# Columns of a folded layer norm inside the main matmuls, and the index scores of three row tiles in one go

## The chip, the cores and the metric

The kernel runs on one core of one Trainium2 chip. Six engines matter here: PE (TensorE) multiplies matrices, DVE (VectorE), ACT (ScalarE) and POOL (GpSimd) work on tiles, SP (SyncE) issues most transfers, and the DMA engines move data between HBM and the on-chip memory SBUF. PE writes into PSUM, which has eight banks of 512 float32 columns on 128 partitions. The metric is the device time of one execution in microseconds (us); 2847.55 us is the median of three runs of the kernel before.

## The reference, cut

Two transformer blocks run one after the other over 512 rows of 1024 columns. In the first one every normalized result goes at once into a product:

```python
def layer_norm(x, g, b):
    mu = mean(x); var = mean((x - mu) ** 2)
    return (x - mu) * rsqrt(var + LN_EPS) * g + b

for i in range(2):
    h = layer_norm(ALPHA * h + 0.5 * swiglu(h, w1, w3, w2), ...)
    mix = ab_mixer(h @ ab_w_in) if i == 0 else dsa_mixer(h @ c_w_in)
    h = layer_norm(ALPHA * h + mix @ w_out, ...)
    h = layer_norm(ALPHA * h + 0.5 * swiglu(h, w1, w3, w2), ...)
    h = h + (p[i] @ ple_w_proj[i]) * sigmoid(h @ ple_w_gate[i])
```

The second mixer picks, for each row, the keys that it attends to by an index of eight small heads (`q` and `k` pass through a rotation, "rope", first):

```python
logits = relu(einsum('bthd,bsd->bths', qi, ki))     # 8 heads of 64
score = einsum('bths,bth->bts', logits, wi)         # weighted sum over heads
score = where(causal, score, -inf)
idx = top_k(score, 128)                             # per row
```

The second block (three attentions and 32 experts, of which each row uses two) is not touched.

## The kernel before, in words

Activations lie transposed: eight tiles of 128 channels by 512 rows (`DT` is 8, `P` 128, `S` 512). Every float32 product is made of three matmuls: each operand is split into a high part and the rest (`hi`, `lo`), and `mm3` (L261 to L263) adds high x high, high x low and low x high in a PSUM bank. `w` loads a weight of 128 x 1024, ScalarE casts the high part (L238), DVE, or POOL where `low` says so, subtracts it (L239); both go into rings of six.

`first_products` is called six times: at the start of the two mixers, in the two second feed-forwards (`ffn`) and in the two gates (`ple`). It starts four products before the layer norm of their input is known. `gained` has prepared `G`, the input times the gain as a pair of tiles, one pair for each of the eight channel tiles. A `part(i, k)` is the product of output i with channel tile k: three matmuls of 512 columns into `out[i]` and two small ones (L412, L413), with the gain and bias vectors themselves as moving columns (four and two), into a shared bank `cs`. `pair(0)` runs outputs 0 and 1 over k, with the sums of the norm (L312, L313: 16 matmuls of one column) after k = 3. DVE turns the sums into the factors of the norm (`rstd`, `rsqrt`: L324 to L356, L338), builds two diagonal tiles from them (L372), and `spread` multiplies these by ones (L374), so that the factors stand in a row for all partitions; ScalarE copies that out (L375). `pair(2)` runs outputs 2 and 3. `corrected` puts the norm in after the fact: out times the first row (L433), and the column sums from `cs` (L436 on ScalarE, L437 on DVE) times the second row added (L439). `normed` makes the normalized input itself, `H`, as pairs (L391, L392, L393, L394), for the products that follow.

In `c_mixer` the generator `index` makes the scores of row tiles 3, 2 and 1 (512, 384 and 256 keys): for each of eight heads a matmul (L1041), a rectifying ScalarE operation into an SBUF tile (L1043) and a multiply-add on DVE (L1045, L1047), then sixteen rounds of top-k on DVE (L1054, L1055). It is interleaved with ten projections and their rope: per projection a ScalarE copy (L970), a shuffle on DVE (L971) and three products on POOL (L973 to L975). From the third projection on, two steps of `index` follow each. The heads (L1084, L1127, L1144) need the result.

The instructions of each engine run in the order in which a scheduler has put the program's; engines meet by semaphores. Buffers come from pools: `self.t()` is one of `SLOTS` (53) tiles of 256 KB, `self.bank()` one of eight PSUM banks. At the end of the program the experts' weights are loaded into the same slots, by SP, in order (L1622, L1625 are its waits there).

Of the kernel before, what the change touches and what calls it, by code (L numbers as in the profile page):

```python
# [9 lines left out]
F32 = mybir.dt.float32  # L10
F32R = mybir.dt.float32r
I32 = mybir.dt.int32
BF16 = mybir.dt.bfloat16
AF = mybir.ActivationFunctionType
ALU = mybir.AluOpType
# [4 lines left out]
S = 512  # L20
D = 1024
DT = D // P
# [27 lines left out]
C_I32, C_BASE, C_TOK, C_I128 = 640, 672, 736, 768  # L50
SLOTS, RING, S5_STEP = 53, 6, 2
CAP, NCOL, NPAIR, NEXT = 64, 32, 16, 16
# [87 lines left out]
class K:  # L140
# [236 lines left out]

    def gained(self, y, g):

        nc, (hi, lo) = self.nc, (self.t(F32R), self.t(F32R))  # L380
        gain = self.vec[:, g:g + 1]
        nc.scalar.activation(hi, y, AF.Copy, scale=gain)  # L382
        nc.vector.scalar_tensor_tensor(lo, y, gain, hi.bitcast(F32), op0=ALU.mult, op1=ALU.subtract)
        return hi, lo
# [12 lines left out]
    def first_products(self, ws, norm, late=False, use=None):  # L397
# [6 lines left out]
        ws, n = list(ws), 4  # L404
        cs, out = self.bank(), [self.bank() for _ in range(n)]

        def part(i, k):
            s = slice(k * P, (k + 1) * P)
            hi, lo = (w[:, s] for w in ws[i])
            v, at = self.gains[:, 4 * (g - V_LNG + k):], 8 * i  # L410
            self.mm3(out[i], (hi, lo), G[k], k == 0, k == DT - 1)
            mm(cs[:, at:at + 4], hi, v[:, :4], start=i == 0 and k == 0, stop=False)  # L412
            mm(cs[:, at:at + 2], lo, v[:, :2], start=False, stop=i == n - 1 and k == DT - 1)  # L413
            self.last_mm = self.mark()
# [14 lines left out]
        def corrected():  # L429
            res, c, ts = [], self.sm(8 * n), []  # L430
            for o in out:
                t = self.t()
                nc.vector.tensor_tensor(t, o, rows[0], ALU.mult)  # L433
                ts.append(t)
            v = lambda t: t[:, :8 * n].rearrange("p (i c) -> p i c", c=8)
            nc.scalar.copy(v(c)[:, :, 2:4], v(cs)[:, :, 2:4])  # L436
            nc.vector.tensor_tensor(v(c)[:, :, 0:2], v(cs)[:, :, 0:2], v(c)[:, :, 2:4], ALU.add)  # L437
            for i, t in enumerate(ts):
                nc.vector.scalar_tensor_tensor(t, rows[1], c[:, 8 * i:8 * i + 1], t, op0=ALU.mult, op1=ALU.add)  # L439
                res.append((t, c[:, 8 * i + 1:8 * i + 2]))  # L440
                if use:
                    use(i, *res[-1])
            return res
# [21 lines left out]
    def ffn(self, X, H, i, ln, then=None, ws=None):  # L465
# [4 lines left out]
        for pi, (a, b) in enumerate(FF_PARTS):  # L470
# [31 lines left out]
            for d in range(DT):  # L502
# [5 lines left out]
                if last:  # L508
                    G.append(self.gained(Y[d], V_LNG + ln * 8 + d))
                    self.stat_add(st, Y[d])  # L510
                    if d == 1 and then:
                        then()
# [16 lines left out]
    def mix_out(self, X, wname, xs, ln, low=None):  # L529
        nc, st, Y, G = self.nc, {}, [], []  # L530
        for d in range(DT):
# [3 lines left out]
            Y.append(y)  # L535
            G.append(self.gained(y, V_LNG + ln * 8 + d))
            self.stat_add(st, y)
        return Y, (Y, G, st, V_LNG + ln * 8, V_LNB + ln * 8)

    def ple(self, X, norm, i, g=None):  # L540
# [13 lines left out]
        for d in range(DT):  # L554
# [10 lines left out]
            if g is not None:  # L565
                HY.append(self.gained(y, g + d))
                self.stat_add(st, y, mean=False)
            else:
                HY.append(self.split(y))
# [418 lines left out]
    def c_mixer(self, X, H):  # L988
# [44 lines left out]
        def index():  # L1033
            for j in (3, 2, 1):
                n = (j + 1) * P
                acc = self.t()[:, :n]
                for h in range(8):
# [3 lines left out]
                    nc.tensor.matmul(o[:, :n], q[rs, j * P:(j + 1) * P], ki[rs, :n], start=True, stop=True)  # L1041
                    r = self.t()
                    nc.scalar.activation(r[:, :n], o[:, :n], AF.Relu)  # L1043
# [25 lines left out]
        for n, _ in enumerate(self.rounds([self.rope(product, ra, sh_a, 32, (nc.gpsimd, nc.gpsimd), qk, n) for n in range(10)], 1)):  # L1069
            for _ in range(2 if n > 1 else 0):  # L1070
                next(idx, None)
# [945 lines left out]
```

## Time and profile before

| what | value |
|---|---|
| median of three runs | 2847.55 us (2846.9 to 2848.05) |
| the profiled execution | 2847.58 us |
| its span, first to last instruction | 2845.8 us |
| PE busy | 2721.4 us, 96% |
| DVE busy | 1545.7 us, 54% |
| ACT busy | 998.7 us, 35% |
| POOL busy | 238.5 us, 8% |
| mean granted clock of PE | 0.968 |

Busy time is the time in which at least one instruction of the engine runs. Matmuls are pipelined, so the records of two that follow one another overlap: their pace is read from the distance of their starts, not from the length of one. The granted clock is 1 at 2.4 GHz and 0.5 at 1.2 GHz. In a row of the timeline the bracket at the end is the idle time of the engine ahead of it and the instruction that ended it.

### The profile page before, as it was taken

Reading aid. Unit: us, or ns where it says so; the run is one execution under the profiler, and the core shown is the slowest. Engines: PE = TensorE matmul, PEld = TensorE weight load, DVE = VectorE, ACT = ScalarE, POOL = GpSimd, SP = SyncE. Lnnn points to the kernel's source line nnn. Section 1 sums busy time; section 2 is a strip of 40 time slices with the busy share of each in tenths; the row PEclk is TensorE's granted clock in tenths of the full one; section 3 lists DMA queues with packets and bytes.
Section 4 is the critical chain, followed back from the end, with each engine's and each line's share of the span. In section 5 each row is a group of like instructions: output and inputs, shape, how many; then the busy total and the mean of one; then the engine's idle time right before and its main releaser. Section 6 shows DMA issues by size and latency. Waiting matters only on the chain. (4 is left out here: it accounts for less than half of the span.)

```text
span 2845.8 us, 34267 instructions
## 1 busy us (share of the span) xinstructions
PE 2721.4 (96%) x13091; PEld 2130.7 (75%) x13091; DVE 1545.7 (54%) x2873; ACT 998.7 (35%) x1634; POOL 238.5 (8%) x250
## 2 busy tenths in 40 slices
PE   9999999999999999999996799999999999969996
PEld 7888878888888878888875588888887777754443
DVE  6856364565333564333579765333578766553435
ACT  5332243334222363222342434222356544322111
POOL 2101001000000000000025000000014222010000
PEclk9999998999999999999998899999999999989998
DMA  6434215423233323223220223232223222669993
GB/s 216 160 109 143 91 58 165 157 93 104 95 98 92 100 78 104 95 91 97 88 104 23 74 67 111 94 99 89 94 100 106 95 74 83 220 208 369 405 410 138
DMA packets 123814, 369.97 MB, mean 130 GB/s; under 512 B 14592, under 2 KB 14656, under 8 KB 123648
## 3 DMA queue, kind: packets, MB, share of 16 engines
q1 hardware_dynamic: 112688, 333.10, 35.1%
q0 software_dynamic: 10384, 33.61, 3.0%
q8 instruction: 103, 1.69, 0.2%
q10 hardware_dynamic: 576, 1.05, 0.1%
q14 instruction: 63, 0.52, 0.1%
HBM read 343.32 MB, written 24.39 MB: 129 GB/s over the span
## 5 line engine op out<-in xcount | busy, mean ns | idle before, releaser
L261 PE MATMUL p<-a,wh 128*128 128x512 f32 x3008 | 1197.4, 399 | 9.4 <-ACT a L551 5.7
L262 PE MATMUL p<-a,wh 128*128 128x512 f32 x3008 | 1178.1, 392 | 1.2 <-DVE a L394 1.2
L263 PE MATMUL p<-a,wl 128*128 128x512 f32 x3008 | 1176.4, 391 | 0.0
L238 ACT CAST wh<-wr 128x1024 fp32r<-128x1024 f32 (+2 forms) x399 | 409.5, 1033 | 1114.4 <-PE p L262 736.5
L261 PEld LDWEIGHTS p<-a,wh 128*128 128x128 f32 x3008 | 569.6, 189 | 135.2 <-issue 7.1
L263 PEld LDWEIGHTS p<-a,wl 128*128 128x128 f32 x3008 | 568.5, 189 | 120.4 <-issue 0.2
L262 PEld LDWEIGHTS p<-a,wh 128*128 128x128 f32 x3008 | 569.5, 189 | 117.7 <-issue 2.6
L239 DVE TENSOR_TENSOR wl<-wr,wh 128x1024 fp32r<-128x1024 f32 (+2 forms) x394 | 471.8, 1201 | 330.2 <-ACT wh L238 319.6
L497 DVE TENSOR_TENSOR a<-a,p 128x512 f32<-128x512 f32 x84 | 57.8, 688 | 262.1 <-PE p L263 244.5
L507 DVE SCALAR_TENSOR_TENSOR a<-p,a 128x512 f32<-128x512 f32 x96 | 66.3, 691 | 192.7 <-PE p L263 192.7
L787 POOL DMA_DIRECT2D spill<-a x76 | 42.6, 562 | 1410.0 <-DVE a L563 556.8
L1134 ACT ACTIVATE a<-a,s 128x256 f32<-128x256 f32 (+3 forms) x128 | 67.4, 528 | 95.3 <-DVE s L1132 95.1
L256 DVE TENSOR_TENSOR a<-a,a 128x512 fp32r<-128x512 f32 x128 | 88.6, 698 | 16.4 <-ACT a L255 16.0
L255 ACT CAST a<-a 128x512 fp32r<-128x512 f32 x128 | 78.5, 622 | 28.8 <-DVE a L563 10.5
L391 DVE TENSOR_TENSOR a<-a,a 128x512 f32<-128x512 f32 x96 | 60.0, 685 | 13.6 <-ACT a L375 13.6
L1846 PE MATMUL p<-we,a 128*64 128x512 f32 x288 | 63.7, 592 | 0.0
L1885 PE MATMUL p<-a,sel 128*128 128x512 f32 x256 | 61.0, 394 | 0.1
L382 ACT ACTIVATE a<-a,vec 128x512 fp32r<-128x512 f32 x56 | 40.5, 723 | 54.0 <-DVE a L507 27.9
L1869 ACT ACTIVATE a<-p,wgt 128x512 fp32r<-128x512 f32 x32 | 22.0, 689 | 103.6 <-PE p L1867 100.0
L1127 DVE CUSTOM_DVE_ANT_0 a<-p,a 128x256 f32<-128x256 f32 (+3 forms) x120 | 50.4, 462 | 11.3 <-PE p L1283 11.0
L1885 PEld LDWEIGHTS p<-a,sel 128*128 128x128 f32 x256 | 47.3, 188 | 11.0 <-issue 0.8
L1886 DVE TENSOR_TENSOR a<-a,p 128x512 f32<-128x512 f32 x72 | 48.4, 686 | 12.6 <-PE p L1885 12.2
(442 smaller groups left out, 2561.3 us busy)
## 6 DMA issues: line engine op xcount, KB each, us to landing
wr<-in_w_dram SPq DMA_DIRECT2D x204, 512.0 KB, 3.4
we<-in_wgu_dram SPq DMA_DIRECT2D x72, 512.0 KB, 9.4
wr<-in_w_dram SPq DMA_DIRECT2D x64, 448.0 KB, 3.3
a<-in_wgu_dram SPq DMA_DIRECT2D x112, 256.0 KB, 5.6
spill<-a POOLq DMA_DIRECT2D x76, 256.0 KB, 2.5
a<-spill SPq DMA_DIRECT2D x76, 256.0 KB, 6.0
we<-in_wd_dram SPq DMA_DIRECT2D x36, 512.0 KB, 11.2
wr<-in_win_dram SPq DMA_DIRECT2D x31, 512.0 KB, 3.8
```

What stands on the lines that cost most here:

```text
L238: nc.scalar.copy(hi[:, :n], raw[:, :n])
L239: (low or nc.vector).tensor_tensor(lo[:, :n], raw[:, :n], hi[:, :n].bitcast(F32), ALU.subtract)
L255: self.nc.scalar.copy(hi[:, :n], x)
L256: (low or self.nc.vector).tensor_tensor(lo[:, :n], x, hi[:, :n].bitcast(F32), ALU.subtract)
L261: mm(o, l[0], r[0], start=start, stop=False)
L262: mm(o, l[0], r[1], start=False, stop=False)
L263: mm(o, l[1], r[0], start=False, stop=stop)
L391: nc.vector.tensor_tensor(y, y, row, op)
L507: nc.vector.scalar_tensor_tensor(Y[d], o, 0.5, Y[d], op0=ALU.mult, op1=ALU.add)
L1134: nc.scalar.activation(s[x], s[x], AF.Exp, bias=nm[:, x:x + 1], accum_out=z[:, x:x + 1])
L1846: nc.tensor.matmul(o[CAP * i:CAP * i + CAP], xT[k // 4][:, a:a + CAP], wg[k], start=k == 0, stop=k == DT - 1)
L1885: nc.tensor.matmul(o, sels[b][:n, j * P:(j + 1) * P], y[h][i][:n], start=b + i == 0, stop=i == 1 and b == len(blocks) - 1)
```

## The change

Norm columns. `gained` now makes its high part as two tiles of 512 columns: `first` holds columns 0 to 255 of the product and, at 256 to 259, the four gain and bias columns, which POOL copies there; the other half goes into a tile that two consecutive channel tiles share. The low part stays one tile. A `part` is six matmuls: three into `out[i]` (260, 256 and 258 columns, so that the four sums come out behind the first 256 columns) and three of 256 columns into a half of a second bank, shared by two outputs. The small matmuls and the bank `cs` are gone; six banks instead of five are held. `corrected` works output by output: two multiplications of 256 columns, a copy of two columns (L454), an addition, the multiply-add. The gate that feeds the second block keeps the old `gained` under the name `gained_rms`. `SLOTS` goes from 53 to 58, for which the room of the descriptors of software DMA is halved.

Index. The rectified scores stay in PSUM (`r = o`), where DVE reads them; and all three row tiles' scores are made behind the second projection, before the third, instead of two tiles behind the third and one behind the fourth.

```diff
-SLOTS, RING, S5_STEP = 53, 6, 2
+SLOTS, RING, S5_STEP = 58, 6, 2
...
-    def gained(self, y, g):
+    def gained(self, y, g, G):
+        nc = self.nc
+        first, lo = self.t(F32R), self.t(F32R)
+        second = G[-1][3] if len(G) % 2 else self.t(F32R)
+        room = second[:, len(G) % 2 * 256:len(G) % 2 * 256 + 256]
+        gain = self.vec[:, g:g + 1]
+        nc.gpsimd.tensor_copy(first[:, 256:260], self.gains[:, 4 * (g - V_LNG):4 * (g - V_LNG) + 4])
+        for hi, s in ((first[:, :256], slice(0, 256)), (room, slice(256, S))):
+            nc.scalar.activation(hi, y[:, s], AF.Copy, scale=gain)
+            nc.vector.scalar_tensor_tensor(lo[:, s], y[:, s], gain, hi.bitcast(F32), op0=ALU.mult, op1=ALU.subtract)
+        G.append((first, room, lo, second))
+
+    def gained_rms(self, y, g):
         nc, (hi, lo) = self.nc, (self.t(F32R), self.t(F32R))
...
-        cs, out = self.bank(), [self.bank() for _ in range(n)]
+        out, second = [self.bank() for _ in range(n)], [self.bank() for _ in range(n // 2)]
+        place = lambda i: second[i // 2][:, i % 2 * 256:i % 2 * 256 + 256]
...
-            self.mm3(out[i], (hi, lo), G[k], k == 0, k == DT - 1)
-            mm(cs[:, at:at + 4], hi, v[:, :4], start=i == 0 and k == 0, stop=False)
-            mm(cs[:, at:at + 2], lo, v[:, :2], start=False, stop=i == n - 1 and k == DT - 1)
+            wh, wl = (w[:, s] for w in ws[i])
+            a, b, lo, _ = G[k]
+            o, begin, end = out[i], k == 0, k == DT - 1
+            mm(o[:, :260], wh, a[:, :260], start=begin, stop=False)
+            mm(o[:, :256], wh, lo[:, :256], start=False, stop=False)
+            mm(o[:, :258], wl, a[:, :258], start=False, stop=end)
+            o, begin, end = place(i), begin and i % 2 == 0, end and i % 2 == 1
+            mm(o, wh, b, start=begin, stop=False)
+            mm(o, wh, lo[:, 256:], start=False, stop=False)
+            mm(o, wl, b, start=False, stop=end)
             self.last_mm = self.mark()
...
-            res, c, ts = [], self.sm(8 * n), []
-            for o in out:
-                t = self.t()
-                nc.vector.tensor_tensor(t, o, rows[0], ALU.mult)
-                ts.append(t)
...
-            nc.scalar.copy(v(c)[:, :, 2:4], v(cs)[:, :, 2:4])
-            nc.vector.tensor_tensor(v(c)[:, :, 0:2], v(cs)[:, :, 0:2], v(c)[:, :, 2:4], ALU.add)
...
+            for i in range(n):
+                t, c = self.t(), self.sm(4)
+                nc.vector.tensor_tensor(t[:, :256], out[i][:, :256], rows[0][:, :256], ALU.mult)
+                nc.vector.tensor_tensor(t[:, 256:], place(i), rows[0][:, 256:], ALU.mult)
+                nc.scalar.copy(c[:, 2:4], out[i][:, 258:260])
+                nc.vector.tensor_tensor(c[:, 0:2], out[i][:, 256:258], c[:, 2:4], ALU.add)
+                nc.vector.scalar_tensor_tensor(t, rows[1], c[:, 0:1], t, op0=ALU.mult, op1=ALU.add)
+                res.append((t, c[:, 1:2]))
...
-                    r = self.t()
+                    r = o
                     nc.scalar.activation(r[:, :n], o[:, :n], AF.Relu)
...
-            for _ in range(2 if n > 1 else 0):
+            for _ in range((0, 3)[n] if n < 2 else 2):
                 next(idx, None)
...
-    nc = bacc.Bacc("TRN2", target_bir_lowering=False, num_devices=1)
+    nc = bacc.Bacc("TRN2", target_bir_lowering=False, num_devices=1, dynamic_dma_scratch_size=8192)
```

Three places show what the change does to the order in which instructions stand on an engine. The first is PE at the start of `pair(0)` in the `ab_mixer` stage. In the kernel before, with `a_2828` and `a_2829` the pair of channel tile 0, `wh_3095` and `wl_3096` the weight of output 0, `p_3118` the bank `cs`:

```order
L261 MATMUL p_3119<-a_2828,wh_3095 128x512
L262 MATMUL p_3119<-a_2829,wh_3095 128x512
L263 MATMUL p_3119<-a_2828,wl_3096 128x512
L412 MATMUL p_3118<-gains,wh_3095 128x4
L413 MATMUL p_3118<-gains,wl_3096 128x2
L261 MATMUL p_3120<-a_2828,wh_3101 128x512
```

And now, with `a_2828` the first half and the four columns, `a_2830` the second half, `a_2829` the low part, `p_3150` the second bank:

```order
L426 MATMUL p_3146<-a_2828,wh_3123 128x260
L427 MATMUL p_3146<-a_2829,wh_3123 128x256
L428 MATMUL p_3146<-a_2828,wl_3124 128x258
L430 MATMUL p_3150<-a_2830,wh_3123 128x256
L431 MATMUL p_3150<-a_2829,wh_3123 128x256
L432 MATMUL p_3150<-a_2830,wl_3124 128x256
L426 MATMUL p_3147<-a_2828,wh_3129 128x260
```

Five matmuls have become six, none of them small. In the kernel before, the 32 small ones of `pair(2)` all stood between the end of `pair(0)` and the spread (L374); now nothing does.

The second place is ScalarE in the same stage, behind the copies of the spread rows. In the kernel before (L392 makes the normalized tiles, L878 and L806 belong to the mixer and use the outputs, L393 casts the first `H`):

```order
L375 COPY a_3244<-p_3243 128x512
L392 ACTIVATE a_258<-a_258,vec 128x512
L392 ACTIVATE a_260<-a_260,vec 128x512
L392 ACTIVATE a_262<-a_262,vec 128x512
L392 ACTIVATE a_264<-a_264,vec 128x512
L392 ACTIVATE a_266<-a_266,vec 128x512
L392 ACTIVATE a_268<-a_268,vec 128x512
L392 ACTIVATE a_270<-a_270,vec 128x512
L878 ACTIVATE a_3343<-a_3332,s_3331 128x512
L878 ACTIVATE a_3346<-a_3334,s_3331 128x512
L878 ACTIVATE a_3349<-a_3336,s_3331 128x512
L806 COPY wr_3422<-p_3423 64x512
```

L878 for the fourth output and then L393 follow. Now, from the last L405 (the former L392) on, where `p_3148` and `p_3149` are the banks of outputs 2 and 3 and L895, L823, L406 are the former L878, L806, L393:

```order
L405 ACTIVATE a_270<-a_270,vec 128x512
L454 COPY s_3411<-p_3148 128x2
L823 COPY wr_3496<-p_3497 64x512
L405 ACTIVATE a_272<-a_272,vec 128x512
L823 COPY wr_3496<-p_3503 64x512
L895 ACTIVATE a_3417<-a_3410,s_3411 128x512
L454 COPY s_3420<-p_3149 128x2
L831 COPY wr_3553<-wr_3496 64x1024
L238 CAST wh_3591<-wr_3590 128x1024
L895 ACTIVATE a_3426<-a_3419,s_3420 128x512
L406 CAST a_3428<-a_258 128x512
```

The first cast of `H` stands, before and now, behind work on the outputs of `pair(2)`; the small copies of each output (L454) have come into this row.

The third place is DVE where the index begins. In the kernel before three shuffles of the rope stand ahead of the scores, which read SBUF tiles (`a_10977` and so on, which ScalarE has written):

```order
L971 STREAM_SHUFFLE a_10895<-a_10894 32x512
L971 STREAM_SHUFFLE a_10933<-a_10932 32x512
L971 STREAM_SHUFFLE a_10971<-a_10970 32x512
L1045 TENSOR_SCALAR a_10974<-a_10977,s_10845 128x512
L1047 SCALAR_TENSOR_TENSOR a_10974<-a_10982,s_10845,a_10974 128x512
```

Now two stand there, and the scores read PSUM banks (`p_`):

```order
L988 STREAM_SHUFFLE a_11191<-a_11190 32x512
L239 TENSOR_TENSOR wl_11199<-wr_11197,wh_11198 128x1024
L988 STREAM_SHUFFLE a_11229<-a_11228 32x512
L1062 TENSOR_SCALAR a_11232<-p_11233,s_11141 128x512
L1064 SCALAR_TENSOR_TENSOR a_11232<-p_11237,s_11141,a_11232 128x512
```

The third shuffle now stands behind the scores of all three row tiles and the first two rounds of top-k.

## Rows read from the trace of the kernel before

**Rows 1.** The page, part 1: busy time, share and instructions of each engine.

```profile
PE 2721.4 (96%) x13091; PEld 2130.7 (75%) x13091; DVE 1545.7 (54%) x2873; ACT 998.7 (35%) x1634; POOL 238.5 (8%) x250
```

**Rows 2.** Windows of the six stages: us; busy of PE, PEld, DVE, ACT, POOL; PEclk, DMA.

```profile
380.54:418.48 37.94, 37.48 (x181) 30.59 (x179) 22.84 (x53) 10.85 (x16) 1.63 (x3) 0.87 0.20 70
...
sum 219.33, PE 218.87 PEld 180.85 DVE 136.00 ACT 73.08 POOL 4.88; mean PE 36.48 PEld 30.14 DVE 22.67 ACT 12.18 POOL 0.81
```

**Rows 3.** Timeline of PE, `pair(0)` of the first stage: start, length, instruction.

```profile
381.36 0.48 PE L261 MATMUL p<-a,wh 128*128 128x512 f32 x1
381.68 0.40 PE L262 MATMUL p<-a,wh 128*128 128x512 f32 x1
381.91 0.39 PE L263 MATMUL p<-a,wl 128*128 128x512 f32 x1
...
382.28 0.48 PE L261 MATMUL p<-a,wh 128*128 128x512 f32 x1
...
387.76 0.36 PE L312 MATMUL p<-ones,a 128*128 128x1 f32 x2
```

**Rows 4.** Timeline of PE, first stage: burst of small matmuls and the spreads.

```profile
398.45 0.25 PE L412 MATMUL p<-gains,wh 128*128 128x4 f32 x1
...
403.35 2.06 PE L374 MATMUL p<-a,ones 128*128 128x512 f32 x2
405.86 1.87 PE L374 MATMUL p<-a,ones 128*128 128x512 f32 x2 [0.46 <-DVE a L372]
```

**Rows 5.** Timeline of PE, matmuls of 264 columns in `c_mixer`.

```profile
1454.81 0.28 PE L261 MATMUL p<-wh,a 128*128 128x264 f32 x1
...
1455.30 0.28 PE L261 MATMUL p<-wh,a 128*128 128x264 f32 x1
```

**Rows 6.** The page, part 5: busy and mean ns of a group, then idle time before.

```profile
L238 ACT CAST wh<-wr 128x1024 fp32r<-128x1024 f32 (+2 forms) x399 | 409.5, 1033 | 1114.4 <-PE p L262 736.5
L261 PEld LDWEIGHTS p<-a,wh 128*128 128x128 f32 x3008 | 569.6, 189 | 135.2 <-issue 7.1
```

**Rows 7.** Timeline of DVE, first stage: factors of the norm, and the two diagonals.

```profile
389.72 0.16 DVE L324 TENSOR_SCALAR s<-p 128x4 f32<-128x4 f32 x1 [4.81 <-PE p L313]
...
394.04 0.87 DVE L372 TENSOR_SCALAR a<-const,s 128x128 f32<-128x128 f32 x4
403.72 0.17 DVE L437 TENSOR_TENSOR s<-p,s 128x8 f32<-128x8 f32 x1 [8.81 <-ACT s L436]
...
404.94 0.87 DVE L372 TENSOR_SCALAR a<-const,s 128x128 f32<-128x128 f32 x4
```

**Rows 8.** Timeline of PE, first stage: the first product with `H`.

```profile
422.50 0.49 PE L261 MATMUL p<-a,wh 128*128 128x512 f32 x1 [2.19 <-ACT a L393]
```

**Rows 9.** Timeline of DVE, `c_mixer`: shuffles of the rope and the scores.

```profile
1483.88 0.72 DVE L971 STREAM_SHUFFLE a<-a 32x512 f32<-32x512 f32 x1
...
1490.00 4.33 DVE L1045 TENSOR_SCALAR a<-a,s 128x512 f32<-128x512 f32 x1
1494.44 12.68 DVE L1047 SCALAR_TENSOR_TENSOR a<-a,s,a 128x512 f32<-128x512 f32 x7
...
1509.88 3.50 DVE L1047 SCALAR_TENSOR_TENSOR a<-a,s,a 128x384 f32<-128x384 f32 x5
...
1515.93 6.53 DVE L1047 SCALAR_TENSOR_TENSOR a<-a,s,a 128x256 f32<-128x256 f32 x7
```

**Rows 10.** Timeline of PE, `c_mixer`: the wait ahead of the heads.

```profile
1580.59 2.47 PE L1567 MATMUL p<-const,a 128*128 128x128 f32 x10 [41.45 <-DVE a L1144]
```

**Rows 11.** Timeline of DVE and POOL in the second block, working at one time.

```profile
2151.83 3.54 POOL L1254 TENSOR_TENSOR a<-a,old 128x512 f32<-128x512 f32 x2 [23.28 <-DVE old L1243]
...
2154.81 0.69 DVE L256 TENSOR_TENSOR a<-p,a 128x512 fp32r<-128x512 f32 x1 [0.59 <-ACT a L255]
```

**Rows 12.** Waits of SP's queue ahead of the experts: what for, total, times, longest.

```profile
SPq L1622 <- DMA hfd<-a: 13.4, 1, 13.4
```

**Rows 13.** The page, part 2: GB/s that DMA moved, in 40 slices.

```profile
GB/s 216 160 109 143 91 58 165 157 93 104 95 98 92 100 78 104 95 91 97 88 104 23 74 67 111 94 99 89 94 100 106 95 74 83 220 208 369 405 410 138
```

More of the change, by code (lines that the diff above doesn't have):

```diff
@@ L404, in first_products @@
         ws, n = list(ws), 4
-        cs, out = self.bank(), [self.bank() for _ in range(n)]
+        out, second = [self.bank() for _ in range(n)], [self.bank() for _ in range(n // 2)]
+        place = lambda i: second[i // 2][:, i % 2 * 256:i % 2 * 256 + 256]
         def part(i, k):
             s = slice(k * P, (k + 1) * P)
-            hi, lo = (w[:, s] for w in ws[i])
-            v, at = self.gains[:, 4 * (g - V_LNG + k):], 8 * i
-            self.mm3(out[i], (hi, lo), G[k], k == 0, k == DT - 1)
-            mm(cs[:, at:at + 4], hi, v[:, :4], start=i == 0 and k == 0, stop=False)
-            mm(cs[:, at:at + 2], lo, v[:, :2], start=False, stop=i == n - 1 and k == DT - 1)
+            wh, wl = (w[:, s] for w in ws[i])
[8 more added lines that the diff above has]
+            mm(o, wl, b, start=False, stop=end)
             self.last_mm = self.mark()
@@ L429, in corrected @@
         def corrected():
-            res, c, ts = [], self.sm(8 * n), []
-            for o in out:
-                t = self.t()
-                nc.vector.tensor_tensor(t, o, rows[0], ALU.mult)
-                ts.append(t)
-            v = lambda t: t[:, :8 * n].rearrange("p (i c) -> p i c", c=8)
-            nc.scalar.copy(v(c)[:, :, 2:4], v(cs)[:, :, 2:4])
-            nc.vector.tensor_tensor(v(c)[:, :, 0:2], v(cs)[:, :, 0:2], v(c)[:, :, 2:4], ALU.add)
-            for i, t in enumerate(ts):
-                nc.vector.scalar_tensor_tensor(t, rows[1], c[:, 8 * i:8 * i + 1], t, op0=ALU.mult, op1=ALU.add)
-                res.append((t, c[:, 8 * i + 1:8 * i + 2]))
+            res = []
+            for i in range(n):
[6 more added lines that the diff above has]
+                res.append((t, c[:, 1:2]))
                 if use:
@@ L508, in ffn @@
                 if last:
-                    G.append(self.gained(Y[d], V_LNG + ln * 8 + d))
+                    self.gained(Y[d], V_LNG + ln * 8 + d, G)
                     self.stat_add(st, Y[d])
@@ L535, in mix_out @@
             Y.append(y)
-            G.append(self.gained(y, V_LNG + ln * 8 + d))
+            self.gained(y, V_LNG + ln * 8 + d, G)
             self.stat_add(st, y)
@@ L565, in ple @@
             if g is not None:
-                HY.append(self.gained(y, g + d))
+                HY.append(self.gained_rms(y, g + d))
                 self.stat_add(st, y, mean=False)
```

## The prediction

> **What bounds the kernel now.** I read the busy times first: PE, the matrix engine, is busy for 96% of the span [rows 1], so in most of the program what PE issues is the time. That share is a mean, and the change touches two kinds of place, so I then read those two. In the six runs of `first_products` the windows from the first matmul on `G` to the last matmul of `pair(2)` add to 219.33 us, with PE busy for 218.87 of it, and the granted clock of the first of them is 0.87 [rows 2]: PE is the limit there, and runs part of the time at 1.2 instead of 2.4 GHz. The timeline of PE in the first window shows what the time is made of. Matmuls of 512 columns start 227 ns apart (381.68, 381.91); one `part`, three of these and two small ones, repeats every 0.92 us (381.36, 382.28) [rows 3]. Three times 0.227 is 0.68, so the two small matmuls, six columns together, take 0.24 us of each part. For `pair(2)` the small matmuls stand in a burst of their own, since they need no `G`: 32 of them from 398.45 to 403.35, 4.9 us, and only then the first spread [rows 4]. The last things to read in this stage are the waits around it: DVE waits 8.81 us for the ScalarE copy of `cs` and with it the second diagonal (404.94) [rows 7], and behind `pair(2)` PE waits 2.19 us for the first normed `H` [rows 8].
>
> The other place is the index of `c_mixer`. There PE is not the limit: it waits 41.45 us for DVE before the heads [rows 10], so the time is what DVE does from the third shuffle on: scores, then sixteen rounds of top-k. The scores of the first row tile are the odd rows: 4.33 us for one multiplication of 512 columns, 12.68 for the seven behind it, while five of 384 columns take 3.50 a little later [rows 9]. POOL runs rope and weight splits at that time.
>
> **The change part by part.** *The parts of the six stages.* Removed: two small matmuls in each of 32 parts of a stage. Three matmuls become six of 256 to 260 columns. The nearest row is the one of 264 columns with the same 128x128 weights: five starts within 1454.81 to 1455.30, 0.122 us apart [rows 5]. Six of these are 0.73 us; by columns (258 of 264) 0.71. I take 0.71; the bounds are 0.68, three of 512 columns, and 0.73. `pair(0)`, 16 parts, goes from 16 x 0.92 = 14.7 to 11.4 us. `pair(2)` goes from 16 x 0.68 = 10.9 to 11.4, which is a loss of 0.5. The burst, 4.9 us in the first stage, is gone. The low clock in the windows is another part: 14.7 + 1.8 for the sums (387.76 to the DVE row at 389.72) + 4.9 + about 3.6 for spreads and the wait between them + 10.9 = 35.9, of 37.94 [rows 2, 3, 4, 7]; the 2 us left over is matmuls of `pair(0)` at 1.2 GHz. The granted clock falls there behind the one-column sums and inside the burst. I take it that without the small ones it stays up.
>
> *What is late next in a stage.* With T0 the first matmul: the sums stand after eight parts, at T0 + 5.7 to 7.5. DVE's chain from the first `rstd` step to the end of the first diagonal takes 389.72 to 394.91 [rows 7], 5.2 us, so the first spread may start at T0 + 12.9, while PE gets to it at 11.4 + 1.8 = 13.2: hidden, with 0.3 to spare. The second diagonal stands in DVE's row behind one split of a new weight (L239), which needs the cast of that weight (L238, 1.03 us [rows 6]) into a ring slot that only the end of `pair(0)` frees. So: 13.2 + 1.03 + 1.22 for the split (403.72 to 404.94) + 0.87 for the diagonal [rows 7] = 16.3. The small copies that stood in this row too (L436 and L437) are gone. The second spread ends 0.9 later (half of the 1.87 that two took at the low clock [rows 4]), at 17.2, and `pair(2)` at T0 + 28.6. Six stages: 219.33 - 6 x 28.6 = 47.7 us.
>
> *What of it is given back.* PE then needs `H`, and ScalarE casts the first `H` behind work on the outputs of `pair(2)` (the order above shows it): this wait moves with the end of `pair(2)` and does not grow by the whole gain. But `corrected` is now longer: per output two multiplications instead of one, a copy on ScalarE and an addition on DVE, for the last two outputs some 4 x 0.2 us and two handovers. I take 1.0 us in each stage, 6 in all; the bounds of one stage are 0 and 4 (the whole chain of spread, product, cast late by half of what PE gained). So the stages give 41.7.
>
> *`gained`.* Two halves on ScalarE and DVE for one each and a POOL copy of four columns, 48 times. They stand behind the last product of the stage before, where DVE and ScalarE wait for PE; POOL has 8% busy time [rows 1] and no queue at these places. PE takes tile k of `G` at T0 + 1.4k, and the last one has 10 us. Nothing, and 0.3 us each stage if this cover were gone.
>
> *Index.* Three things. The scores start behind the second shuffle (ends at 1484.6), not the third (which ends where the first score starts, 1490.0): 5.4 us, less one more shuffle of 0.7 that now comes behind them [rows 9]. Second, the rows themselves: those of 512 columns take 4.33 + 12.68 = 17.0 us, seven of 256 columns 6.53, more than the five of 384 suggest [rows 9]. What ails the long ones is seen where POOL and DVE run together elsewhere: with POOL busy from 2151.83 to 2155.37, a DVE operation of 512 columns with one operand in PSUM takes 0.69 us [rows 11]: it is not stretched. The new score operations read PSUM and one SBUF tile, as that one does. For 512 columns I take 0.80 (between this 0.69 and 3.50 / 5 x 512 / 384 = 0.93, which holds the waits of a chain), 0.50 for 256; 384 stay at 0.70. That is 17.0 - 8 x 0.80 = 10.6 less and 6.53 - 7 x 0.50 = 3.0 less, together 13.6 (12 to 15). Third, PE: its eight remaining projections, 24 matmuls of 0.227 us each, 5.45 us, now start some 12 us later (8 x 2.0 = 16 us of scores, less the eight banks that PE may be ahead, 8 x 0.5), near 1497, and end near 1541; the heads now start at 1580.59, and by this at 1562. PE's wait shrinks to some 21 us and still covers them. Sum: 5.4 - 0.7 + 13.6 = 18.3.
>
> *Slots.* Weights of the experts are loaded into the same slots, and SP waits there, once 13.4 us, for a slot [rows 12] before a stretch in which DMA is the limit at about 410 GB/s [rows 13]. Five more slots of 256 KB are 1.3 MB, 3.2 us at that rate, if all of them are filled earlier. 0 to 3.2; I take 2. The smaller ring for software DMA descriptors I cost at nothing; such transfers are few and far apart here.
>
> *Sum.* The profiled execution took 2847.58 us with a span of 2845.8, the median of the runs is 2847.55: the same. 2847.6 - 41.7 - 18.3 - 2 = 2785.6; I say **2786**.
>
> **The rivals.** *Given back behind `pair(2)`.* The DVE and ScalarE rows of `corrected` and `normed`, not PE, set when the next products can start. For it: PE waits for `H` already now [rows 8], and this row is not shorter than before. Against it: the first spread comes at T0 + 13.2 instead of 22.8 (403.35 less 380.54 [rows 2, 4]), and those rows can begin with it. If half is lost, 3.5 us more in each stage: 2786 + 21 = **2807**.
>
> *The scores are still slow.* They go on PE's, ScalarE's or POOL's pace, and the 13.6 us are not had, only the earlier start: **2800**. For it: in no row of before does a chained multiply-add with a PSUM operand run beside POOL's shuffled rope; against it: [rows 11].
>
> *Weight loads set the pace, and the kernel becomes slower.* Six loads instead of five, and half as many columns behind each to hide one. A load's record is 189 ns long [rows 6]. Should each matmul wait for its own, a part is 6 x 0.189 = 1.13 us: `pair(0)` is then 3.4 us longer, `pair(2)` 7.2, the burst saves 4.9, so +5.7 a stage and +34 in all, against 20.3 from index and slots: **2861**. It decides the sign from about 0.176 us a matmul on, where 32 parts of 1.06 us less the 30.5 that parts and burst take now are 3.4 us a stage, 20.3 in all. Against it stands 0.122 at 264 columns [rows 5], with loads as large as these. The Trainium skill has a rule that speaks for this rival (TensorE: Matmul & The Clock Gate, section The mechanism): a weight load overlaps with matmuls in flight only where it goes to another group of rows, and these loads take all rows. By its prices (sections LDWEIGHTS and Back-to-back issue gap) a load of 128 is 107 ns and a matmul of 256 columns 109, so by estimate 216 ns each and 1.30 us a part, and the sum near 2895. This case's trace does not agree: at 0.122 the load is hidden.
>
> *Better than forecast.* The low clock behind PE's waits for `H` goes too, nothing is given back, and all slots count: 47.7 + 20 + 3.2 and some 3 for the clock, **2774**.
>
> *The change does nothing*, if the small matmuls had only filled time in which PE would have waited for the first spread: 2845. Against it: [rows 3], where the 0.24 us lie between full matmuls.
>
> **How the numbers follow.** Forecast 2786: 0.60. Given back, 2807: 0.18. Scores slow, 2800: 0.12. Better, 2774: 0.05. Weight loads, 2861: 0.03. Nothing: 0.02. The range from 2771 to 2810 takes in the first four with the bounds of their terms, and leaves out the other two and the case in which two losses add (about 2820). A difference under 0.2%, 5.7 us, is about what a measurement of this kernel can't tell from none. Faster 0.95, same 0.02, slower 0.03.
>
> **What would show it.** Right: in the new PE timeline parts of 0.71 us with starts 0.118 apart, no burst, windows of 28 to 29.5 us each, clock near 1 in them; the first score at the second shuffle, scores of 512 columns under 1 us with POOL busy, and PE's wait before the heads at 20 to 25 us. Wrong: starts 0.16 or more apart; a wait for `H` of more than 5 us behind `pair(2)`; DVE waiting in the score chain for ScalarE or PE; low clock in the windows all the same.

## The result, and the profile after

The changed kernel took 2785.35 us (median of four runs, 2784.17 to 2786.86) against 2847.63 us: a ratio of 0.9782, with a 95% interval from 0.9765 to 0.9799. Its profiled run took 2784.83 us, with a span of 2782.9.

The same windows as in [rows 2], from the first matmul on `G` to the last of `pair(2)`, in the changed kernel (length in us; busy time of PE, PEld, DVE, ACT, POOL with the number of instructions; granted clock, DMA share, GB/s):

```profile
379.92:408.05 28.13, 26.60 (x213) 25.29 (x212) 23.17 (x58) 12.28 (x20) 1.62 (x3) 1.00 0.29 95
...
sum 168.97, PE 159.59 PEld 151.68 DVE 138.99 ACT 81.56 POOL 4.86; mean PE 26.60 PEld 25.28 DVE 23.16 ACT 13.59 POOL 0.81
```

Together 168.97 us for 219.33. The clock is 1.00 in all six. What stands in a window is seen in the timeline of PE in the first of them, which answers to [rows 3] and [rows 4]:

```profile
390.98 0.28 PE L426 MATMUL p<-a,wh 128*128 128x260 f32 x1
391.10 0.28 PE L427 MATMUL p<-a,wh 128*128 128x256 f32 x1
...
391.69 0.28 PE L426 MATMUL p<-a,wh 128*128 128x260 f32 x1
...
393.12 1.02 PE L374 MATMUL p<-a,ones 128*128 128x512 f32 x2
395.67 1.13 PE L374 MATMUL p<-a,ones 128*128 128x512 f32 x2 [1.53 <-DVE a L372]
396.24 0.68 PE L426 MATMUL p<-a,wh 128*128 128x260 f32 x1
...
414.20 0.80 PE L261 MATMUL p<-a,wh 128*128 128x512 f32 x1 [5.11 <-ACT a L406]
```

A part is 0.71 us (390.98 to 391.69), the first spread starts 13.20 us after the window does, the second waits 1.53 us for DVE, and `pair(2)` begins at T0 + 16.3. The last row answers to [rows 8]: behind `pair(2)` PE now waits 5.11 us for `H`, where it waited 2.19 (and 1.0 more in three short waits beside that row).

The index, as DVE ran it (answers to [rows 9]):

```profile
1448.49 0.71 DVE L988 STREAM_SHUFFLE a<-a 32x512 f32<-32x512 f32 x1
1449.11 0.72 DVE L1062 TENSOR_SCALAR a<-p,s 128x512 f32<-128x512 f32 x1
1449.93 4.17 DVE L1064 SCALAR_TENSOR_TENSOR a<-p,s,a 128x512 f32<-128x512 f32 x5
...
1456.61 2.42 DVE L1065 TENSOR_TENSOR a<-a,const 128x128 f32<-128x128 f32 x1
...
1473.53 0.01 DVE L988 LOAD_MASK_SELECT a<-a  x1 [1.23 <-ACT a L987]
```

And PE ahead of the heads (answers to [rows 10]):

```profile
1529.79 2.47 PE L1584 MATMUL p<-const,a 128*128 128x128 f32 x10 [15.25 <-DVE a L1161]
```

The multiply-adds of 512 columns, 1.8 us each in the kernel before, are 0.83 us apart. From the end of the window in `c_mixer` to the heads it is 112.35 us (1417.44 to 1529.79) instead of 128.02 (1452.57 to 1580.59).

Where the 62.9 us of the span went can be read by laying the matmuls of the two traces side by side. The start of the first window is 0.6 us earlier. The six windows give 9.8, 7.9, 9.4, 9.4, 6.1 and 7.8 us, in sum 50.4. Between the first and the second window 2.1 us are lost again (1.2 in the trace of the repeated run of this kernel below), and between the others that don't hold the index 0.9 more are gained in sum. The stretch with the index, up to the fifth window, gives 15.1. Behind the sixth window 2.0 are lost: 2.1 more are gained right behind it, 2.4 are lost in the attentions of the second block, and 1.6 before the experts, where PE waits for the first gather of rows. That wait was 7.47 us before; in the trace of the changed kernel it is this row:

```profile
2492.82 1.97 PE L1849 MATMUL p<-const,wr 128*128 128x128 f32 x8 [9.10 <-DMA wr<-hfd,toki]
```

Through the whole stretch of the experts the two traces then run at one distance, 62.8 to 63.0 us.

### The profile page after: what moved, and what is told of

Same layout as the page of the kernel before. It is cut to its first block, busy times and chain, and to the rows that moved or that the text cites. A ratio compares the mean times of both kernels' runs of the same rounds, so it can differ in the third digit from the quotient of the medians.

```text
span 2782.9 us, 34941 instructions
## 1 busy us (share of the span) xinstructions
PE 2670.1 (96%) x13283; PEld 2104.5 (76%) x13283; DVE 1543.1 (55%) x2963; ACT 1007.5 (36%) x1700; POOL 251.2 (9%) x298
## 5 line engine op out<-in xcount | busy, mean ns | idle before, releaser
L261 PE MATMUL p<-a,wh 128*128 128x512 f32 x2816 | 1107.4, 394 | 10.7 <-ACT a L406 5.1
L262 PE MATMUL p<-a,wh 128*128 128x512 f32 x2816 | 1101.0, 391 | 0.1
L263 PE MATMUL p<-a,wl 128*128 128x512 f32 x2816 | 1099.3, 391 | 0.0
L239 DVE TENSOR_TENSOR wl<-wr,wh 128x1024 fp32r<-128x1024 f32 (+2 forms) x394 | 472.8, 1203 | 322.0 <-ACT wh L238 312.4
L261 PEld LDWEIGHTS p<-a,wh 128*128 128x128 f32 x2816 | 531.6, 189 | 129.3 <-ACT a L568 5.5
L263 PEld LDWEIGHTS p<-a,wl 128*128 128x128 f32 x2816 | 531.1, 189 | 111.5 <-issue 0.2
L262 PEld LDWEIGHTS p<-a,wh 128*128 128x128 f32 x2816 | 531.4, 189 | 110.1 <-DVE a L407 1.4
L514 DVE TENSOR_TENSOR a<-a,p 128x512 f32<-128x512 f32 x84 | 57.7, 687 | 260.0 <-PE p L263 252.0
L386 POOL CAST a<-gains 128x4 fp32r<-128x4 f32 x48 | 15.7, 327 | 1221.0 <-PE p L262 890.9
L256 DVE TENSOR_TENSOR a<-a,a 128x512 fp32r<-128x512 f32 x128 | 87.1, 685 | 15.7 <-ACT a L255 15.4
L388 ACT ACTIVATE a<-a,vec 128x256 fp32r<-128x256 f32 x96 | 43.7, 501 | 43.5 <-DVE a L524 26.5
L426 PE MATMUL p<-a,wh 128*128 128x260 f32 x192 | 57.5, 300 | 0.0
L1144 DVE CUSTOM_DVE_ANT_0 a<-p,a 128x256 f32<-128x256 f32 (+3 forms) x120 | 50.4, 463 | 11.4 <-PE p L1300 11.0
```

The source lines that it names most:

```text
L239: (low or nc.vector).tensor_tensor(lo[:, :n], raw[:, :n], hi[:, :n].bitcast(F32), ALU.subtract)
L256: (low or self.nc.vector).tensor_tensor(lo[:, :n], x, hi[:, :n].bitcast(F32), ALU.subtract)
L261: mm(o, l[0], r[0], start=start, stop=False)
L262: mm(o, l[0], r[1], start=False, stop=False)
L263: mm(o, l[1], r[0], start=False, stop=stop)
```

## The experiments

The runs come from three chips, and medians of different chips are compared by their ratio to the kernel before. That kernel took 2849.21 us on the chip of the two halves, of the first run without small matmuls and of the slots; 2845.0 on the chip of the diagonals alone, of the two edits of the index and of the mask; and 2845.77 on the chip of the other four runs.

**The two halves apart.** The first kernel is the changed one with the old index:

```diff
-                    r = o
+                    r = self.t()
...
-            for _ in range((0, 3)[n] if n < 2 else 2):
+            for _ in range(2 if n > 1 else 0):
```

> The changed kernel with the index as it was: scores rectified into SBUF tiles, two row tiles behind the third projection and one behind the fourth. Theory A (the two halves of the change add up, as the shifts of PE between the traces say: some 15.7 us from the end of the pair of products in c_mixer to the heads, the rest from the six stages): 2785.4 + 15.7 = 2801 us, the six windows 28.1 us each as in the changed kernel, PE's wait ahead of the heads 41 us again. Rival B (the terms of the prediction: 41.7 from the stages and 2 from the slots): 2804 us, windows of 28.1 but waits for H behind them that are about 1 us longer in each stage.

Measured: 2802.75 us, ratio 0.9835 (0.9819 to 0.9852). The windows are 28.1 us each. The second is the kernel before with the two lines of the index changed the other way:

> The kernel before with the new index alone (rectified in PSUM, all three row tiles behind the second projection). Theory A: 2847.6 - 15.7 = 2832 us; the score operations of 512 columns 0.85 us apart with POOL busy. Rival B (the prediction's term, 18.3): 2829 us. Rival C (the index gain needs the free slots or the earlier start of the changed kernel): 2840 us or more.

Measured: 2832.12 us, ratio 0.9932 (0.9912 to 0.9952). 46.5 us and 17.1 us less than the 2849.21 on this chip add to 63.6; the change as a whole gave 62.3. So far as these medians tell (the four runs of the second kernel lie between 2824.92 and 2834.0) the halves are independent, and theory A holds within 2 us for both.

**What the small matmuls cost.** The kernel before without them; the column sums of the norm are left out and set to zero:

```diff
-            mm(cs[:, at:at + 4], hi, v[:, :4], start=i == 0 and k == 0, stop=False)
-            mm(cs[:, at:at + 2], lo, v[:, :2], start=False, stop=i == n - 1 and k == DT - 1)
...
+            nc.vector.memset(c, 0.0)
```

> The kernel before without the 64 small matmuls of each stage; the norm's column sums are left out (set to zero), so part of the norm is missing. It prices the small matmuls alone: three of 512 columns remain. Theory A (they cost their place between full matmuls, their burst, and the low clock): windows of 12.7 + 1.03 + 1.22 + 0.87 + 0.5 + 10.9 = 27.2 us each, granted clock 1.00 in them, 163 in sum for 219.3; in time about 2847.6 - 56 + 3 = 2795 us. Rival D (the low clock comes from the one-column sums, which stay): clock under 0.95 in the windows, 29 us or more each, 2805 us. Rival E (they only filled waits for the spread): windows over 33 us, 2830 us or more.

Measured: 2808.2 us, ratio 0.9855 (0.9838 to 0.9871); windows of 29.7 to 32.0 us. The granted clock is 0.94 in five windows and 0.89 in one. Theory A and rival E miss; the figures are those of rival D, but not its cause: behind the one-column sums the matmuls start 0.23 us apart, at the high clock. The small matmuls are most of the gain (41 us), but the kernel that leaves them out is slower than the one that carries their columns along, 2802.75 on the same chip. The timeline shows why. First DVE, then PE in the first window:

```profile
392.07 1.22 DVE L239 TENSOR_TENSOR wl<-wr,wh 128x1024 fp32r<-128x1024 f32 x1 [1.63 <-ACT wh L238]
393.21 0.15 DVE L338 TENSOR_TENSOR s<-s,s 128x4 f32<-128x4 f32 x1
393.28 0.87 DVE L372 TENSOR_SCALAR a<-const,s 128x128 f32<-128x128 f32 x4
```

```profile
394.21 3.64 PE L374 MATMUL p<-a,ones 128*128 128x512 f32 x4 [2.40 <-DVE a L372]
```

The scheduler put the split of the next weight (L239) ahead of the last step of the factors (L338) this time, so that both spreads wait for it: PE stands still for 2.40 us, and runs the spreads and the next matmul at the low clock (0.56 over those 3.8 us). The same split stands between the two diagonals in the changed kernel. A last run takes both steps: no small matmuls, and both diagonals built one behind the other:

> The kernel before without the small matmuls (the norm's column sums left out, set to zero) and with both diagonals built ahead of the split. In the run without small matmuls alone the windows were 30.3 us and PE waited 2.4 us for the diagonals, with the low clock behind that wait. Theory A (that wait is the split's, and the low clock the wait's): windows of 10.9 + 1.8 + 1.7 + 10.9 = 25.3 us, granted clock 1.00, time 2808.2 - 30 + 5 to 15 given back = 2783 to 2793 us. Rival B (the low clock belongs to the sums, or the wait to the factors): windows of 27 us or more, clock 0.95 or less.

Measured: 2798.87 us, ratio 0.9835 (0.9819 to 0.9851). The first window:

```profile
381.06:409.07 28.01, 25.61 (x117) 20.29 (x115) 21.54 (x51) 9.72 (x13) 1.63 (x3) 1.00 0.28 94
```

PE is busy for 25.61 us of 28.01 and waits 2.40, again for the split, which stayed ahead of L338; the edit had moved only the diagonals. So the expected 25.3 us is what PE works, not what the window lasts, and rival B was right on the length. The clock is 1.00 in five of the six windows, as theory A has it. In time the kernel now stands where the one with the new norm alone stands, by the ratios (0.9835 for both). What this settles is the price: without small matmuls a window holds 25.6 us of work, and with the six matmuls of the changed kernel 26.6; 16 parts of 0.71 us instead of 0.68 are 0.5 us for each of the two pairs.

**Both diagonals ahead of the split**, in the changed kernel:

```diff
-        rows = [self.spread(c) for c in self.rm]
+        rows = self.spreads(self.rm)    # both dg first, then matmul and copy of each
```

> The changed kernel, with both diagonal tiles built ahead of the weight split that stands between them on DVE. Theory A (PE's wait of 1.5 us between the spreads is that split's): the second spread follows the first at once, windows of 26.3 us instead of 28.1, and in all 5 to 11 us less, 2774 to 2780 us. Rival B (what waits then is the next weight or H, so that the windows get shorter and the time between them longer): 2784 us. Rival C (PE waits for the factors themselves, not for the split): windows unchanged.

Measured: 2779.75 us (2775.23 to 2780.14), ratio 0.9762 (0.9745 to 0.9778). All windows are alike, and PE doesn't wait in them:

```profile
380.93:407.26 26.33, 26.33 (x213) 25.37 (x212) 22.16 (x56) 11.88 (x19) 1.62 (x3) 1.00 0.30 101
...
sum 157.98, PE 157.98 PEld 152.17 DVE 131.90 ACT 77.94 POOL 4.31; mean PE 26.33 PEld 25.36 DVE 21.98 ACT 12.99 POOL 0.72
```

The windows give 11.0 us, and some 6 arrive (2779.75 against 2785.35; by the ratios 5.7, or 7 beside the repeated run below). In four of the six stages PE waits longer behind the window: 5.57 us instead of 5.11 in the first, 3.47 for 2.43 in the third, 1.83 for 0.89 in the fourth, 2.77 for 2.26 in the sixth. So both theories hold a part, A for the window, B for what follows it.

**Is it `H` behind the outputs?** The last question was asked with a kernel that joins three edits, and the same with the normalized `H` made ahead of the corrected outputs everywhere (`late=True`). The three edits are the diagonals, the causal mask in the first multiplication (next paragraph), and this order of the index:

```diff
-            for _ in range((0, 3)[n] if n < 2 else 2):
+            for _ in range((0, 2)[n] if n < 2 else 2):
```

The changed kernel itself was run beside them:

> The changed kernel itself, on the chip of the following runs, as their measure. 2785 us; every theory expects the same.

Measured: 2784.6 us, ratio 0.9787 (0.9771 to 0.9804).

> Three edits on the changed kernel: both diagonals ahead of the split, the mask in the first multiplication, and two row tiles' scores behind the second projection and the third's behind the third (so that PE gets to the third projection sooner). Theory A (the first is worth 5.5 us as measured; the mask addition's 2.1 us beside POOL and the wait for the third projection, 1.2 and with the mask moved 2.7 us, then both go): 2785.4 - 5.5 - 3.3 = 2776.5 us, the wait under 0.5 us. Rival B (the third projection is late whatever the order, since PSUM banks hold PE back): 2779.8 us, the wait still 1 us or more.

Measured: 2775.68 us (2774.36 to 2780.61), ratio 0.9755 (0.9738 to 0.9773), 8.9 us under the changed kernel on the same chip: the fastest of all by its median. The runs with the diagonals alone cover the same range, so nothing is shown for the other two edits: DVE still waits for the third projection, 3.37 us, and the heads start 114.45 us behind the window, where it is 114.09 with the diagonals alone (112.35 in the changed kernel; 0.94 of the difference is a longer wait behind the window). The wait is as rival B has it.

> As the run before, with the normalized H made ahead of the corrected outputs in all six stages (it was so in the feed-forwards only). In the run with both diagonals PE waits behind the pair of products for 5.6 us in the first mixer, 3.5 and 2.8 in the two gates, 1.8 in the second mixer. Theory A (these waits are H standing behind the corrected outputs on ScalarE and DVE): they shrink by half or more, 6 to 10 us less than the run before, 2768 us. Rival B (then the corrected outputs are what PE waits for, or the PSUM banks that they hold): the waits move, and the time is within 3 us of the run before or above it.

Measured: 2777.06 us, ratio 0.9761 (0.9745 to 0.9777). PE's wait in the first mixer and in the first gate:

```profile
413.66 1.92 PE L838 MATMUL p<-const,a 128*64 128x128 f32 x8 [6.40 <-ACT s L470]
```

```profile
995.23 0.76 PE L261 MATMUL p<-a,wh 128*128 128x512 f32 x1 [4.71 <-DVE s L471]
```

Rival B, in three of the four stages: there the waits moved from the cast of `H` to the small copies and additions of the corrected outputs (L470, L471) and grew, from 5.59 us to 6.40 in the first mixer and from 3.47 and 2.78 to 4.7 in the gates. Whichever of the two DVE and ScalarE make first there, PE waits for the other. In the second mixer the wait of 1.83 us is gone, and from the window to the heads it is 111.81 us instead of 114.45. The times of the two kernels are not told apart.

**The index, its two edits apart.** In the changed kernel, the first with SBUF tiles again:

```diff
-                    r = o
+                    r = self.t()
```

> The changed kernel, with the scores rectified into SBUF tiles again (the early place of all three row tiles stays). Theory A (a DVE operation with two SBUF operands is held by POOL, one with a PSUM operand is not): the multiply-adds of 512 columns 1.6 us and more with POOL busy, the scores some 9 us longer, 2785.4 + 9 = 2794 us. Rival B (what counts is the early place and that PE is ahead): scores in 20 to 22 us as in the changed kernel, 2786 us.

Measured: 2792.57 us, ratio 0.9813 (0.9797 to 0.983). The same five multiply-adds:

```profile
1449.49 16.45 DVE L1064 SCALAR_TENSOR_TENSOR a<-a,s,a 128x512 f32<-128x512 f32 x5
1466.40 1.61 DVE L1064 SCALAR_TENSOR_TENSOR a<-a,s,a 128x512 f32<-128x512 f32 x2 [0.46 <-DVE a L1064]
```

And POOL, which is busy without a gap from 1449.16 on; its last row ends at 1465.39:

```profile
1457.84 7.55 POOL L239 TENSOR_TENSOR wl<-wr,wh 128x1024 fp32r<-128x1024 f32 x3
```

16.45 us instead of 4.17, with nothing changed but where one operand lies; and the two multiply-adds that come when POOL is done take 0.8 us each, as with PSUM. Theory A. The second has PSUM, and the old places:

> The changed kernel, with two row tiles' scores behind the third projection and one behind the fourth again (PSUM stays). Theory A (one projection of 5.45 us is waited for in the chain, less a shuffle of 0.7): 2785.4 + 4.7 = 2790 us. Rival B (in the changed kernel DVE waits 1.2 us for the third projection behind the first rounds of top-k, which this order doesn't, and one wide multiplication beside POOL is avoided): 2787 us or less.

Measured: 2792.6 us, ratio 0.9812 (0.9796 to 0.9828). From the end of the window to the heads, the four combinations are: 112.35 us as changed, 118.82 (PSUM, old places), 121.06 (SBUF, new places) and 130.82 (SBUF, old places, the first run above). Early places give 6.5 to 9.8 us, PSUM 8.7 to 12.0. Of the second kernel's loss 6.5 us lie there, more than the 4.7 of theory A. DVE still meets POOL's hold (the mask's addition takes 1.62 us) and waits 1.54 us for the fourth projection before the last row tile; what makes up the difference was not worked out.

**The mask's addition**, 2.42 us in the changed kernel where its like takes 0.28:

```diff
-                        nc.vector.tensor_scalar(acc, r[:, :n], wi[j][:, h:h + 1], None, op0=ALU.mult)
+                        nc.vector.tensor_scalar(acc[:, :n - P], r[:, :n - P], wi[j][:, h:h + 1], None, op0=ALU.mult)
+                        stt(acc[:, n - P:n], r[:, n - P:n], wi[j][:, h:h + 1], cm, op0=ALU.mult, op1=ALU.add)
...
-                tt(acc[:, n - P:n], acc[:, n - P:n], cm, ALU.add)
```

> The changed kernel, with the causal mask added in the first multiplication of each row tile (PSUM operand) instead of in an addition of its own of two SBUF operands, which took 2.42 us once beside POOL. Theory A (that addition held the chain): 2 to 2.5 us less, 2783 us. Rival B (DVE waits for the third projection right behind, 1.2 us now, and this wait takes all of it): 2785.4 us and a wait there of 3 us.

Measured: 2783.49 us, ratio 0.9777 (0.9761 to 0.9794). The long addition is gone, and the wait behind it is longer:

```profile
1473.43 0.01 DVE L988 LOAD_MASK_SELECT a<-a  x1 [2.72 <-ACT a L987]
```

2.72 us for 1.23; from the window to the heads it is 111.20 us, 1.15 less. By the rows mostly rival B, though the time is the one that theory A names; a gain of that size is not told apart in the times.

**The slots.** The kernel before with 58 slots and the smaller ring:

```diff
-SLOTS, RING, S5_STEP = 53, 6, 2
+SLOTS, RING, S5_STEP = 58, 6, 2
...
-    nc = bacc.Bacc("TRN2", target_bir_lowering=False, num_devices=1)
+    nc = bacc.Bacc("TRN2", target_bir_lowering=False, num_devices=1, dynamic_dma_scratch_size=8192)
```

> The kernel before with 58 slots and the smaller ring of descriptors, nothing else. Theory A (the deeper prefetch of expert weights stands in the way of the first gather, whose wait grew from 7.47 to 9.10 us between the traces): 2847.6 + 1.6 = 2849.2 us, with that wait at 9 us. Rival B (the prediction's term): 2845.6 us. Rival C (neither; the longer wait has another cause): 2847.6 us and a wait of 7.5.

Measured: 2848.64 us beside 2849.21, ratio 0.9997 (0.9983 to 1.001). The time decides between none of the three. The traces say more. PE's wait for the first gather is 8.5 us here, 7.5 before and 9.0 to 9.1 in the changed kernel's; over all the traces of this document it is 7.0 to 8.0 us in the four kernels with 53 slots and 8.2 to 9.6 in the ten with 58. That is theory A's wait. And the attentions of the second block, of which no theory spoke, are longer with 58 slots: from PE's first matmul of L1307 to that of L1726, where the experts' part begins, it is 358.75 us before and 361.25 here (357.5 to 358.9 in the four kernels, 360.3 to 361.5 in the ten). The largest part of it is one wait of PE, first before, then here:

```profile
2220.39 1.12 PE L1307 MATMUL p<-a,a 128*64 128x128 f32 x6 [3.04 <-ACT a L1301]
```

```profile
2216.65 1.12 PE L1307 MATMUL p<-a,a 128*64 128x128 f32 x6 [4.70 <-ACT a L1301]
```

POOL prepares additive tiles for these attentions, and they lie in slots. Before, it gets to them at 2216.61. Here it does so while DVE still works on the factors of the softmax that PE waits for:

```profile
2203.22 4.02 POOL L1253 TENSOR_SCALAR a<-old 128x512 f32<-128x512 f32 x2 [14.80 <-DVE s L1127]
2207.31 2.54 POOL L1254 TENSOR_TENSOR a<-a,old 128x512 f32<-128x512 f32 x2
```

```profile
2208.62 1.25 DVE L1139 TENSOR_TENSOR s<-s,s 128x4 f32<-128x4 f32 x1 [2.04 <-ACT s L1138]
```

This operation on four columns ends with POOL's row, at 2209.87; it takes 0.16 us before, with POOL idle. Two like it ahead of it (L1131, L1132) take 0.58 and 0.57 us for 0.17 and 0.16. The three make 1.9 us: what happened to the scores happens here to small operations. From the gather to the end the two traces are equally long, so that nothing is gained there. By the traces this edit costs some 3.5 us (2.5 in the attentions, 1.0 ahead of the gather), a little more than the interval of the ratio allows; part of it may be made up elsewhere. Whether the longer wait for the gather comes from the slots or from the smaller ring, no run separates.

## Why the prediction was right, and where only its sum was

2786 us was forecast and 2785.35 measured. The two large mechanisms are the forecast ones. That the sum is met within a microsecond is luck: against the forecast 62.0 us the windows gave 2.7 us more, 4.8 less was given back, the index gave 3.2 less, slots and attentions together 6.0 less, and 2.7 came from places without a term (0.6 ahead of the first window, 2.1 right behind the sixth).

*Parts and windows: right, the gain a little low.* A part at 0.71 us, the first spread at T0 + 13.2, no burst, and windows of 28.1 us where 28.6 was forecast. The half microsecond has three parts. ScalarE casts the next weight from 392.53 on, T0 + 12.6, before `pair(0)` has ended, so that the second spread starts at T0 + 15.75 and not at 16.3. It holds PE for 0.57 us and not 0.9, which I had taken from a row at the low clock [rows 4]. And `pair(2)` lasts 11.8 us, not 11.4, since 0.52 us pass from the start of its first matmul to that of the second. The windows gave 50.4 us, not 47.7. That the low clock would leave the windows is confirmed in all six.

*Given back behind `pair(2)`: too much by some 5 us.* I took 1.0 us in each stage. Only the first mixer gave some back, 2.1 us (1.2 in the repeated run), where ScalarE casts the first `H` behind the outputs [rows 8]; over the other four that don't hold the index, none. The bound of 0 was nearer. The wait of 5.11 us there is over the 5 us that the prediction names as a sign against itself, in this stage alone. In the gates the wait behind the window became half a microsecond shorter (2.95 to 2.43 us, 2.78 to 2.26).

*Low clock behind the waits for `H`.* The prediction had it go only in its case "better than forecast". It went in one of three places: behind the wait in the second gate the granted clock is 1.00 where it was 0.72, and that, with the shorter wait, is the 2.1 us right behind the sixth window. In the first gate it is 0.70 over the first 5.7 us (0.72 before), and behind the first mixer's wait 0.53 over 5.8 us.

*Index: 2.6 us too much, two waits not seen.* 18.3 us were forecast; from the window to the heads the change gave 15.7, and 15.5 in the kernel before with the new index alone (128.02 to 112.56). In the kernel with the new norm the exchange gives 18.5 (130.82 to 112.35), near the forecast by chance, because the old index is longer there: one multiplication is held for 7.02 us where it was 4.33 [rows 9]. In the changed kernel two things were missing from my list of rows: the mask's addition has two SBUF operands and was held by POOL for 2.1 us, and DVE waits 1.23 us for the third projection, which comes behind the scores on PE. Such a wait of DVE for ScalarE is among the signs that the prediction names against itself. PE's wait ahead of the heads came out at 15.25 us, outside the 20 to 25 that were named as a sign of being right.

*Slots and attentions: wrong in sign.* 2 us were forecast; 4.0 were lost, 2.4 in the attentions, of which no step spoke, and 1.6 in the wait for the first gather. The distance between the traces does not change by more than 0.2 us while the experts run. The term that failed is the step from "SP waits for a slot" [rows 12] to "time is gained": what PE waits for there is the gather, not a weight. And more slots also let POOL begin its work in the attentions earlier, beside DVE: the run with the slots alone shows both losses. In the changed kernel's trace the wait of 3.04 us is 4.69, and a second one of 0.65 stands behind it. The smaller ring was costed at nothing, and that is not shown: no run has it apart from the slots.

*Rivals.* Weight loads as the pace: ruled out, 0.118 us a matmul, with half the columns behind each load. What the row of 264 columns said [rows 5] held. Scores still slow: ruled out by the run that puts them into SBUF again. Given back: in the first stage only, 2.1 of 9.8 us; once the window was shortened further, by both diagonals, nearly half of that further gain was lost behind it.

## What to carry to other kernels

A matmul of a few columns between wide ones costs far more than its columns (0.12 us each here, and 0.15 in a burst that ran in part at 1.2 GHz): where a bank of PSUM has room, let the columns ride on a matmul that runs anyway, even if the wide one has to be halved for it. If DVE works beside POOL, look for operations with two SBUF operands; one operand left in PSUM took the rows here from 3.3 us to 0.83. Multiplications with a single SBUF tensor were held too (4.33 and 7.02 us), and so were operations on four columns, 1.25 us for 0.16, while the steps of top-k were not. More buffers can cost time in the same way: here they let POOL start earlier, and it got into DVE's way. When a stage gets shorter, read what stands in the other engines' rows between its steps: one split of a later weight cost 1.8 us in each of six stages, and moving it gave the largest gain that was left.

## What the runs showed of the hardware that was not expected

The kernel before is not only slower but less steady: on one chip its nine runs lie between 2839.85 and 2852.24 us, with a mean granted clock of 0.971 in the shortest and 0.967 in the longest, while five runs of the changed kernel lie between 2782.97 and 2786.96. The windows of the first stage, cut finer, show where the clock fell in the kernel before:

```profile
380.54:390.30 9.76, 9.76 (x60) 8.64 (x59) 4.51 (x8) 3.14 (x4) 0.00 (x0) 1.00 0.01 2
390.30:393.70 3.40, 3.40 (x11) 2.80 (x10) 2.99 (x14) 0.00 (x0) 0.00 (x0) 0.51 0.24 77
393.70:400.60 6.90, 6.90 (x48) 6.25 (x46) 1.14 (x7) 1.05 (x1) 0.00 (x0) 0.99 0.00 0
400.60:407.40 6.80, 6.34 (x19) 4.07 (x19) 3.42 (x9) 0.76 (x2) 0.00 (x0) 0.50 0.13 34
```

The second and the fourth stretch, at 1.2 GHz, follow a run of very narrow matmuls (sums and parts with small ones; the burst) in which PE was never idle. In the changed kernel the same sums stand between matmuls of 256 columns, and the clock stays at 2.4 GHz in the windows. What makes it fall is not settled by this: with the small matmuls gone it fell behind a wait of 2.40 us in one kernel, and behind waits of 2.0 to 2.4 us in another it did not, in five of six windows.
